# Two layers of a DeltaNet and Conformer encoder: gates stored as sigmoids, running sums one tile sooner, squares, weights and stores moved

## The chip, the core and the metric

The kernel runs on one core of a Trainium2 chip, as one launch. The metric is the device time of one execution in microseconds (us), the median of several runs. TensorE multiplies matrices, VectorE (DVE) and ScalarE (ACT) work on elements, GpSimd (POOL) takes some element work and stores, SyncE (SP) issues most of the loads. ScalarE and GpSimd issue DMAs too, each in the order of its own instructions.

## What is computed

Two layers, each a residual block on x of 2048 tokens by 1024 channels in float32; a final RMSNorm follows. Cut to what matters:

```python
h = rms_norm(x, norm_w)
qkv, z_a, a_lg, b_lg, cf_val, cf_glu, z_b, gate_lg = split(h @ w_in)
qkv = silu(depthwise_conv_centred(qkv, qkv_conv_w))
# 4 heads, both directions, chunked gated delta rule, running sums of g in a chunk
o = o_fwd + o_bwd
y_a = (rms_norm(o, dn_norm_w) * silu(z_a)) @ w_dn_out
u = depthwise_conv_centred(cf_val * sigmoid(cf_glu), cf_conv_w) + cf_conv_b
u = silu(layer_norm(u, cf_ln_w, cf_ln_b))
y_b = (u * silu(z_b)) @ w_cf_out
gate = sigmoid(gate_lg + gate_b)
x = x + (gate[0] * y_a + gate[1] * y_b) @ w_out
```

## The kernel before, in words

Channels lie on partitions, tokens on the free axis, in four blocks of 512. A product by a weight tile of 128 columns is three matmuls for each 128 of depth: weight and activation are each split in a high and a low part (`split`, L158 on ScalarE makes the high part, L159 on VectorE the low one), and L175, L176 and L177 multiply high by high, low by high, high by low. A tile of full depth is thus 24 matmuls of 128x512. TensorE's order is made of such tiles, and other work is put between them.

Each layer has these stages. **Projection**: for each of four heads, `head` makes the tiles of k, q and v with their convolution of five taps (`conv_tiles`: L563 on ScalarE, L565 on VectorE, then SiLU, L552) and `conformer` a tile of the conformer branch (GLU: L725 and L729). The follow-up work of a head is a queue of generators, `post`: at each tile `follow` runs the first of them up to its next `yield`. For head 0 the first is `scalars`, the decays and write strengths: long element work on VectorE (L444 to L470), then the running sums as two products (L475, L477), copied by L479, and their transpose L495. Behind it come `keys` (transposes of k and q, L573, sums of squares, Gram products L628 and L629, and the factors bh, L642) and `values`. Behind those, work of VectorE that is not tied to a tile lies in another queue, `back`, which `pump` feeds at a rate: `solve`, the inverse of the triangular blocks of a head (it starts with the transpose L666 of bh, its copy L668, a store and a load back, then steps L704, L706), and `conformer_conv`, 30 steps of L740.

**Gates**: `gates(0)` makes the 16 gate tiles for the blocks 0 and 1, 32 tiles; ScalarE adds the bias (L820, tile `go`) and stores them to `gt_d` in device memory. `conformer_norm` (L775 to L798) runs beside them. **Scan**: `delta` runs 16 steps of both directions in lockstep; a step has products such as L979 and L982, and `finish` norms and stores the outputs of earlier steps (squares L1034, L1052, L1057, and L1058 on VectorE). Between the parts of a step `pull` takes matmuls out of a `filler`: first `gates(1)` for blocks 2 and 3, then `early_merge`, the conformer's output product for blocks 0 and 1 times its gate: loads of `gt_d` (tile g), the sigmoid L1187 on ScalarE and L1193 on VectorE. The order of the scan is bound on every engine as it is written (`bind`). **Merge**: `merge` takes the other gates from `gt_d` (sigmoid L1247), multiplies, adds and makes the product with w_out; in the first layer L1297 adds x, `add_square` (L228, L231 on ScalarE) sums squares, and SyncE stores the new x (L149); in the second `last_out` does this and closes each block with the final norm.

Elsewhere a scheduler orders the instructions of each engine by their dependencies, so a line that is moved can move others.

Of the kernel before, what the change touches and what calls it, by code (L numbers as in the profile page):

```python
# [6 lines left out]
F32 = mybir.dt.float32  # L7
# [26 lines left out]
PART = 5  # L34
LATE = 4
AHEAD = 4
R2 = 3.7
# [25 lines left out]
def cut(x):  # L63
    return x.rearrange("p (a i) -> p a i", a=2)
# [13 lines left out]
class Trunk:  # L78
# [9 lines left out]

    def bind(self, start):
        last = {}  # L90
        for ins in self.nc.cur_bb.bb.instructions[start:]:
            if ins.engine in BOUND:
                if ins.engine in last:
                    self.tc.add_manual_dep(ins, last[ins.engine], NOSYNC, reason="written order")
                last[ins.engine] = ins.name
# [64 lines left out]

    def weight(self, src, kk):
        hi = self.pw.tile([P, KD, P], F32R, tag="whi", bufs=2, name="whi")[:, 0:kk, :]
        lo = self.pw.tile([P, KD, P], F32R, tag="wlo", bufs=2, name="wlo")[:, 0:kk, :]
        for k in range(0, kk, 4):
            raw = self.pw.tile([P, 4, P], F32, tag="wraw", bufs=2, name="wraw")
            self.load(raw, src[:, k:k + 4, :])
            self.split(hi[:, k:k + 4, :], lo[:, k:k + 4, :], raw)
        return hi, lo

# [256 lines left out]
    def scalars(self, pt):  # L426
# [42 lines left out]
        v_.tensor_copy(dch(self.beta), cdh(n(9)))  # L469
        yield  # L470
        yield
# [329 lines left out]
    def gates(self, half):  # L801
# [5 lines left out]
        for i, (j, b) in enumerate(seq):  # L807
            for q, _ in seq[i:]:
                if q not in ws and len({z for z, _ in seq[i:] if z in ws}) < 2:
                    ws[q] = self.weight(self.a["w_in"][self.l, 28 + q], KD)  # L810
            blk = 2 * half + b
            ps = self.pd()
            for more in self.dense_steps(ps, ws[j], self.hx(blk), KD):
                if more:
                    yield 1
            if self.rate:
                self.follow()
                self.pump(self.rate)
            o = self.st("go")
            nc.scalar.activation(cut(o), sort(ps), AF.Identity, bias=self.vec[:, V_GB + j:V_GB + j + 1])  # L820
            self.astore(self.gt_d[j, :, blk * NB:(blk + 1) * NB], o)
            yield 1

    def delta(self):
# [272 lines left out]
        for step in range(NCH):  # L1097
# [27 lines left out]
            if step == NCH - 1:  # L1125
                break
            next(new)
            pull(STEP[2])
            next(last)
            ready = go(step + 1)  # L1130
# [46 lines left out]
    def early_merge(self, wcf, ahead, seq, gs, gate):  # L1177
        nc = self.nc
        for i, (j, b) in enumerate(seq):
            if b == 0:  # L1180
                wc = ahead
                if j + 1 < KD:
                    ahead = self.weight(wcf[j + 1], 4)
            if i + 2 < len(seq):
                gate(i + 2)
            g = gs.popleft()
            nc.scalar.activation(g, g, AF.Sigmoid)  # L1187
            sl = slice(b * NB, (b + 1) * NB)
# [25 lines left out]
    def merge(self, l, xd, fnw):  # L1214
# [10 lines left out]
        for half in range(2):  # L1225
# [10 lines left out]
            for j in range(KD):  # L1236
# [5 lines left out]
                for b in order:  # L1242
# [3 lines left out]
                    self.load(gt[:, 0:n], self.gt_d.rearrange("(n j) p t -> j p n t", n=2)[j][:, 0:n, tk])  # L1246
                    nc.scalar.activation(gt[:, 0:n], gt[:, 0:n], AF.Sigmoid)  # L1247
                    ys[b] = [gt[:, 0, :], gt[:, 1, :] if half else self.y1[:, j, b * NB:(b + 1) * NB]]
# [28 lines left out]
            for j in range(KD):  # L1277
# [12 lines left out]
                for b in order:  # L1290
# [7 lines left out]
                    self.add_square(ss[:, sl], xn[j][:, sl], j == 0)  # L1298
                    self.store(xnew[j, :, tk], xn[j][:, sl])
                if j + 1 < KD:  # L1300
# [22 lines left out]
    def last_out(self, l, half, xd, fnw, yhi, ylo, ahead, order, w0):  # L1323
# [42 lines left out]
        for b in order:  # L1366
# [15 lines left out]
            for j in range(whole):  # L1382
# [7 lines left out]
                if whole < KD and j and len(ws) < KD - whole:  # L1390
# [3 lines left out]
                    ws.append((hi, lo))  # L1394
            if whole == KD:
                if b == order[0]:
                    w0 = self.weight(a["w_out"][l, 0], KD)
                run(close(o, NB, None))
                continue
# [81 lines left out]
```

## Time and profile before

| | us |
|---|---|
| median of 3 runs | 3178.48 (3176.97 to 3181.95) |
| the profiled execution | 3177.78 |
| its span | 3176.0 |
| TensorE busy | 3087.8 |
| VectorE busy | 2400.1 |
| ScalarE busy | 1382.5 |
| GpSimd busy | 298.4 |

The span goes from the first to the last instruction that the profiler saw. An engine's busy time is the union of its instructions; TensorE's holds the stretches at a lower clock too, which the granted clock (PEclk, a share of full speed) shows. A wait is idle time of an engine, put down to the instruction that ended it.

### The profile page before, as it was taken

To read this page: it belongs to the slowest core of one execution; us is meant where nothing else is said; L and a number is where in the kernel's file an instruction comes from. 1 tells how busy PE (TensorE), PEld (TensorE's weight loads), DVE (VectorE), ACT (ScalarE), POOL (GpSimd) and SP (SyncE) were. 2 spreads that over 40 slices of the span, in tenths; PEclk is the share of its full clock that TensorE was granted. 3 is DMA by queue.
4 is the path that set the end of the run, shared out by engine and by line. 5 is a ranking of instruction groups with operands and counts; after the bars stand their busy time and mean duration, and the time that the engine had idled before them with its cause. 6 is when DMAs were issued, how large, how long until landed. Compare 5 with 4: busy or idle time off the path is not lost. (4 is left out here: it accounts for less than half of the span.)

```text
span 3176.0 us, 51511 instructions
## 1 busy us (share of the span) xinstructions
PE 3087.8 (97%) x19190; PEld 2715.3 (85%) x19190; DVE 2400.1 (76%) x4441; ACT 1382.5 (44%) x3113; POOL 298.4 (9%) x297
## 2 busy tenths in 40 slices
PE   6998999999999999999999999999999999999998
PEld 5887888888889998888888888888888899988887
DVE  7769899997656698746667699998955667877665
ACT  5624252522344466533345332525234445765342
POOL 3000000000022222000000000000001222200000
PEclk9998999999999999999999999999999999999999
DMA  4232323234588787665413141414356878965643
GB/s 145 83 100 70 100 80 101 82 100 161 184 295 251 253 265 226 192 195 135 144 44 114 49 124 64 120 60 120 115 171 231 278 238 265 289 191 188 215 157 126
DMA packets 429418, 501.72 MB, mean 158 GB/s; under 512 B 96432, under 2 KB 262960, under 8 KB 429168
## 3 DMA queue, kind: packets, MB, share of 16 engines
q1 hardware_dynamic: 355840, 388.58, 39.9%
q10 hardware_dynamic: 65264, 80.09, 7.3%
q0 software_dynamic: 8064, 29.76, 2.5%
q8 instruction: 151, 2.47, 0.3%
q14 instruction: 99, 0.81, 0.1%
HBM read 342.74 MB, written 155.58 MB: 157 GB/s over the span
## 5 line engine op out<-in xcount | busy, mean ns | idle before, releaser
L175 PE MATMUL pd<-h,whi 128*128 128x512 f32 x2816 | 1093.7, 389 | 0.0
L177 PE MATMUL pd<-h,wlo 128*128 128x512 f32 x2816 | 1071.5, 381 | 4.9 <-DVE wlo L159 4.9
L176 PE MATMUL pd<-h,whi 128*128 128x512 f32 x2816 | 1072.1, 381 | 0.0
L740 DVE SCALAR_TENSOR_TENSOR cacc<-gp,vec,cacc 128x1009 f32<-128x1009 f32 (+1 forms) x480 | 615.8, 1283 | 31.1 <-ACT cacc L738 28.1
L177 PEld LDWEIGHTS pd<-h,wlo 128*128 128x128 f32 x2816 | 534.7, 190 | 82.6 <-DVE wlo L159 6.5
L175 PEld LDWEIGHTS pd<-h,whi 128*128 128x128 f32 x2816 | 534.7, 190 | 80.0 <-issue 1.4
L176 PEld LDWEIGHTS pd<-h,whi 128*128 128x128 f32 x2816 | 535.4, 190 | 72.9 <-issue 1.9
L158 ACT ACTIVATE whi<-wraw 128x512 fp32r<-128x512 f32 x394 | 240.2, 624 | 451.0 <-PE pd L176 302.9
L159 DVE TENSOR_TENSOR wlo<-wraw,whi 128x512 fp32r<-128x512 f32 x394 | 270.4, 699 | 135.4 <-ACT whi L158 135.0
L565 DVE SCALAR_TENSOR_TENSOR acc<-cin,vec,acc 128x1022 f32<-128x1022 f32 (+1 forms) x192 | 245.7, 1299 | 11.5 <-ACT acc L563 10.5
L177 PE MATMUL pd<-yhi,wlo 128*128 128x512 f32 x488 | 185.7, 381 | 4.5 <-DVE wlo L159 4.5
L175 PE MATMUL pd<-yhi,whi 128*128 128x512 f32 x488 | 185.5, 380 | 1.8 <-ACT whi L158 1.8
L176 PE MATMUL pd<-ylo,whi 128*128 128x512 f32 x488 | 185.0, 379 | 0.0
L820 ACT ACTIVATE go<-pd,vec 128x512 f32<-128x512 f32 x128 | 87.0, 680 | 123.7 <-PE pd L177 101.7
L541 ACT ACTIVATE cin<-pd 128x512 f32<-128x512 f32 x96 | 56.7, 592 | 165.5 <-PE pd L177 165.4
L752 ACT ACTIVATE ao<-pd 128x512 f32<-128x512 f32 x64 | 38.3, 599 | 179.2 <-PE pd L177 174.5
L177 PEld LDWEIGHTS pd<-yhi,wlo 128*128 128x128 f32 x488 | 92.2, 189 | 19.8 <-DVE wlo L159 6.9
L175 PEld LDWEIGHTS pd<-yhi,whi 128*128 128x128 f32 x488 | 92.2, 189 | 15.7 <-ACT whi L158 3.0
L175 PE MATMUL pd<-uop,whi 128*128 128x512 f32 x256 | 100.5, 393 | 3.2 <-ACT dm L1052 3.2
L176 PEld LDWEIGHTS pd<-ylo,whi 128*128 128x128 f32 x488 | 92.2, 189 | 13.0
L176 PE MATMUL pd<-uop,whi 128*128 128x512 f32 x256 | 98.2, 383 | 0.0
L177 PE MATMUL pd<-uop,wlo 128*128 128x512 f32 x256 | 97.8, 382 | 0.0
(311 smaller groups left out, 4837.1 us busy)
## 6 DMA issues: line engine op xcount, KB each, us to landing
wraw<-w_in SPq DMA_DIRECT2D x240, 256.0 KB, 3.5
gt<-go ACTq DMA_DIRECT2D x128, 256.0 KB, 4.1
dl<-gr SPq DMA_DIRECT2D x128, 256.0 KB, 5.3
dl<-kq SPq DMA_DIRECT2D x64, 512.0 KB, 6.4
dl<-kv SPq DMA_DIRECT2D x64, 512.0 KB, 5.8
wraw<-w_out SPq DMA_DIRECT2D x90, 256.0 KB, 3.1
kq<-acc SPq DMA_DIRECT2D x16, 1024.0 KB, 5.3
gr<-go ACTq DMA_DIRECT2D x64, 256.0 KB, 2.2
```

The lines of the kernel that those rows point to most:

```text
L158: self.nc.scalar.activation(hi, src, AF.Copy)
L159: self.nc.vector.tensor_tensor(out=lo, in0=src, in1=hi.bitcast(F32), op=ALU.subtract)
L175: mm(ps, whi[:, k, :], xhi, start=k == 0, stop=False)
L176: mm(ps, whi[:, k, :], xlo, start=False, stop=False)
L177: mm(ps, wlo[:, k, :], xhi, start=False, stop=k == kk - 1)
L541: nc.scalar.activation(cut(t[:, o + b * NB:o + (b + 1) * NB]), sort(ps), AF.Copy)
L565: self.nc.vector.scalar_tensor_tensor(out=out, in0=t[:, k:k + n], scalar=wc(k), in1=out, op0=ALU.mult, op1=ALU.add)
L740: self.nc.vector.scalar_tensor_tensor(out=acc, in0=t[:, k:k + n], scalar=wc(k), in1=acc, op0=ALU.mult, op1=ALU.add)
L752: nc.scalar.activation(cut(o), sort(ps), func)
L820: nc.scalar.activation(cut(o), sort(ps), AF.Identity, bias=self.vec[:, V_GB + j:V_GB + j + 1])
```

## The change

It has six parts. `gates` stores the sigmoid of the gates of blocks 0 and 1, and the two places that read them leave out theirs. In the steps from 12 on, the squares of a pair of outputs are written behind the third `pull`. One of two yields in `scalars` goes. The first w_out tile of a block in `last_out` is written between the parts of the closing norm, whose VectorE order is bound. In `early_merge` the loads of the next w_cf tile and its split are written apart, one for each block. `merge` stores the new x from ScalarE's queue.

```diff
--- before.py
+++ after.py
@@ -33,6 +33,7 @@
 Z = '121'
 PART = 5
 LATE = 4
+LATE_SQUARES = 12
 AHEAD = 4
 R2 = 3.7
 BIG = -1.0e30
@@ -86,10 +87,10 @@
     def mark(self):
         return len(self.nc.cur_bb.bb.instructions)
 
-    def bind(self, start):
+    def bind(self, start, engines=BOUND):
         last = {}
         for ins in self.nc.cur_bb.bb.instructions[start:]:
-            if ins.engine in BOUND:
+            if ins.engine in engines:
                 if ins.engine in last:
                     self.tc.add_manual_dep(ins, last[ins.engine], NOSYNC, reason="written order")
                 last[ins.engine] = ins.name
@@ -158,14 +159,23 @@
         self.nc.scalar.activation(hi, src, AF.Copy)
         self.nc.vector.tensor_tensor(out=lo, in0=src, in1=hi.bitcast(F32), op=ALU.subtract)
 
-    def weight(self, src, kk):
+    def weight_parts(self, src, kk):
         hi = self.pw.tile([P, KD, P], F32R, tag="whi", bufs=2, name="whi")[:, 0:kk, :]
         lo = self.pw.tile([P, KD, P], F32R, tag="wlo", bufs=2, name="wlo")[:, 0:kk, :]
+        raws = []
         for k in range(0, kk, 4):
-            raw = self.pw.tile([P, 4, P], F32, tag="wraw", bufs=2, name="wraw")
-            self.load(raw, src[:, k:k + 4, :])
-            self.split(hi[:, k:k + 4, :], lo[:, k:k + 4, :], raw)
-        return hi, lo
+            raws.append(self.pw.tile([P, 4, P], F32, tag="wraw", bufs=2, name="wraw"))
+            self.load(raws[-1], src[:, k:k + 4, :])
+
+        def split():
+            for k, raw in zip(range(0, kk, 4), raws):
+                self.split(hi[:, k:k + 4, :], lo[:, k:k + 4, :], raw)
+        return (hi, lo), split
+
+    def weight(self, src, kk):
+        w, split = self.weight_parts(src, kk)
+        split()
+        return w
 
     def dense_steps(self, ps, w, xs, kk):
         mm = self.nc.tensor.matmul
@@ -468,7 +478,6 @@
         v_.reciprocal(out=n(9), in_=n(9))
         v_.tensor_copy(dch(self.beta), cdh(n(9)))
         yield
-        yield
         ps = self.pz()
         tri = self.st("tri")[:, 0:256].rearrange("p (d c) -> p d c", d=2)
         v_.tensor_scalar(out=tri, in0=self.con[:, C_MF:C_MB + 1, :], scalar1=0.0, scalar2=None, op0=ALU.is_equal)
@@ -817,7 +826,8 @@
                 self.follow()
                 self.pump(self.rate)
             o = self.st("go")
-            nc.scalar.activation(cut(o), sort(ps), AF.Identity, bias=self.vec[:, V_GB + j:V_GB + j + 1])
+            nc.scalar.activation(cut(o), sort(ps), AF.Identity if half else AF.Sigmoid,
+                                 bias=self.vec[:, V_GB + j:V_GB + j + 1])
             self.astore(self.gt_d[j, :, blk * NB:(blk + 1) * NB], o)
             yield 1
 
@@ -1124,8 +1134,11 @@
             done.clear()
             if step == NCH - 1:
                 break
-            next(new)
+            if step < LATE_SQUARES:
+                next(new)
             pull(STEP[2])
+            if step >= LATE_SQUARES:
+                next(new)
             next(last)
             ready = go(step + 1)
             last = new
@@ -1180,11 +1193,12 @@
             if b == 0:
                 wc = ahead
                 if j + 1 < KD:
-                    ahead = self.weight(wcf[j + 1], 4)
+                    ahead, split = self.weight_parts(wcf[j + 1], 4)
+            elif j + 1 < KD:
+                split()
             if i + 2 < len(seq):
                 gate(i + 2)
             g = gs.popleft()
-            nc.scalar.activation(g, g, AF.Sigmoid)
             sl = slice(b * NB, (b + 1) * NB)
             ps = self.pd()
             for more in self.dense_steps(ps, wc, lambda k: (self.u0[:, k, sl], self.u0[:, 4 + k, sl]), 4):
@@ -1244,7 +1258,8 @@
                     gt = self.hm("gt")[:, 0:2 * NB].rearrange("p (n t) -> p n t", n=2)
                     n = 1 + half
                     self.load(gt[:, 0:n], self.gt_d.rearrange("(n j) p t -> j p n t", n=2)[j][:, 0:n, tk])
-                    nc.scalar.activation(gt[:, 0:n], gt[:, 0:n], AF.Sigmoid)
+                    if half:
+                        nc.scalar.activation(gt[:, 0:n], gt[:, 0:n], AF.Sigmoid)
                     ys[b] = [gt[:, 0, :], gt[:, 1, :] if half else self.y1[:, j, b * NB:(b + 1) * NB]]
                 if half:
                     for b in order:
@@ -1296,7 +1311,7 @@
                     self.load(xr, xd[j][:, tk])
                     v_.tensor_tensor(out=cut(xn[j][:, sl]), in0=sort(ps), in1=cut(xr), op=ALU.add)
                     self.add_square(ss[:, sl], xn[j][:, sl], j == 0)
-                    self.store(xnew[j, :, tk], xn[j][:, sl])
+                    self.astore(xnew[j, :, tk], xn[j][:, sl])
                 if j + 1 < KD:
                     w = self.weight(a["w_out"][l, j + 1], KD)
             if half:
@@ -1393,9 +1408,13 @@
                         self.split(hi[:, k:k + 4, :], lo[:, k:k + 4, :], raws[len(ws)][:, k:k + 4, :])
                     ws.append((hi, lo))
             if whole == KD:
+                c = close(o, NB, None)
+                run(c, 2)
+                start = self.mark()
                 if b == order[0]:
                     w0 = self.weight(a["w_out"][l, 0], KD)
-                run(close(o, NB, None))
+                run(c)
+                self.bind(start, (mybir.EngineType.DVE,))
                 continue
             start = self.mark()
             n = NB // 2
```

Line numbers of the changed kernel are 9 to 14 higher. The places where the instructions move:

VectorE, the running sums of the first layer (`scalars`; abw holds its work, ngc, neg and sig go with the decays), before:

```order
L464 COPY abw<-abw 128x16x2x4
L479 COPY abw<-pz 128x128
L481 COPY abw<-pz 128x128
L483 TENSOR_SCALAR ngc<-abw 128x128
L487 TENSOR_SCALAR neg<-eg 128x128
L490 TENSOR_TENSOR abw<-abw 128x128
L496 COPY abw<-pz 128x128
L159 TENSOR_TENSOR wlo<-wraw,whi 128x512
L498 TENSOR_SCALAR abw<-abw,sig 128x128
```

and now:

```order
L474 COPY abw<-abw 128x16x2x4
L488 COPY abw<-pz 128x128
L490 COPY abw<-pz 128x128
L492 TENSOR_SCALAR ngc<-abw 128x128
L505 COPY abw<-pz 128x128
L507 TENSOR_SCALAR abw<-abw,sig 128x128
L496 TENSOR_SCALAR neg<-eg 128x128
L499 TENSOR_TENSOR abw<-abw 128x128
L574 SCALAR_TENSOR_TENSOR acc<-cin,vec,acc 128x1022 x2
```

The copy of the transposed sums (L496, now L505) and its product come ahead of two splits (L159), and the convolution of the first head follows at once.

VectorE, the start of the first head's solve (L666's result is copied by L668, now L677; sol is the solve's buffer, cacc the conformer's convolution), before:

```order
L740 SCALAR_TENSOR_TENSOR cacc<-gp,vec,cacc 128x1009 x8
L511 MEMSET cin 128x2
L688 TENSOR_TENSOR sol<-gr 128x1024
L511 MEMSET cin 128x2
L693 TENSOR_TENSOR sol<-sol 128x1024
L159 TENSOR_TENSOR wlo<-wraw,whi 128x512 x2
L668 COPY bt<-pz 32x128
L159 TENSOR_TENSOR wlo<-wraw,whi 128x512 x2
L694 TENSOR_TENSOR sol<-sol,br 64x1024
L695 TENSOR_TENSOR sol<-sol,br 64x1024
```

and now:

```order
L651 TENSOR_TENSOR bh<-beta,rk 128x32
L521 COPY gp<-gp 128x30
L653 COPY beta<-bh 128x32
L697 TENSOR_TENSOR sol<-gr 128x1024
L663 TENSOR_TENSOR vo<-pz,vs 128x512 x4
L677 COPY bt<-pz 32x128
L518 MEMSET cin 128x2
L749 SCALAR_TENSOR_TENSOR cacc<-gp,vec,cacc 128x1009 x3
```

The copy stood behind the conformer's first convolution; now it follows bh and the four products vo, and the convolution follows it. On TensorE the transpose L666 stands behind matmul 736 of the layer before and behind matmul 472 now.

ScalarE in the last steps of the scan (oss are the sums of squares, g the gates, dm and dh buffers), before:

```order
L915 ACTIVATE dh_6988<-dh_6988 32x4x32 x4
L1034 ACTIVATE junk,oss<-dm_6984 128x128 x8
L158 ACTIVATE whi<-wraw 128x512
L1187 ACT_TABLE_LOAD
L1187 ACTIVATE g_10748<-g_10748 128x512
L1187 ACTIVATE g_10896<-g_10896 128x512
L988 ACTIVATE dm_6983<-pz,eg 128x128 x8
```

and now:

```order
L925 ACTIVATE dh_6988<-dh_6988 32x4x32 x4
L1044 ACTIVATE junk,oss<-dm_6984 128x128 x8
L159 ACTIVATE whi<-wraw 128x512
L998 ACTIVATE dm_6983<-pz,eg 128x128 x8
L939 ACTIVATE dh_6989<-pz 128x128
L1007 ACTIVATE dm_6983<-pz 128x512 x2
```

The table load and both sigmoids have left; the squares stand where they stood. VectorE at the same place, before:

```order
L917 TENSOR_TENSOR dl_6981<-dl_6981,dm_6982 128x512 x2
L919 TENSOR_TENSOR dl_6981<-dl_6981,dm_6982 128x512 x2
L159 TENSOR_TENSOR wlo<-wraw,whi 128x512
L1193 TENSOR_TENSOR y_11062<-pd,g_10748 128x512
L1058 SCALAR_TENSOR_TENSOR dh_6985<-pz,vec,dh_6985 128x512
L1058 SCALAR_TENSOR_TENSOR dh_6986<-pz,vec,dh_6986 128x512
L961 COPY dl_6981<-pz 64x4x64
L962 COPY dl_6981<-pz 64x4x64
```

and now:

```order
L927 TENSOR_TENSOR dl_6981<-dl_6981,dm_6982 128x512 x2
L929 TENSOR_TENSOR dl_6981<-dl_6981,dm_6982 128x512 x2
L1207 TENSOR_TENSOR y_11053<-pd,g_10739 128x512
L1068 SCALAR_TENSOR_TENSOR dh_6985<-pz,vec,dh_6985 128x512
L1068 SCALAR_TENSOR_TENSOR dh_6986<-pz,vec,dh_6986 128x512
L971 COPY dl_6981<-pz 64x4x64
L972 COPY dl_6981<-pz 64x4x64
L160 TENSOR_TENSOR wlo<-wraw,whi 128x512
```

L1193 (now L1207) is ahead of L159 (now L160), which was ahead of it. On ScalarE's whole order there are 60 table loads before and 85 now.

## Rows read from the trace of the kernel before

**Rows 1.** The page: its first line, and part 1, busy time of each engine.

```profile
span 3176.0 us, 51511 instructions
...
PE 3087.8 (97%) x19190; PEld 2715.3 (85%) x19190; DVE 2400.1 (76%) x4441; ACT 1382.5 (44%) x3113; POOL 298.4 (9%) x297
```

**Rows 2.** TensorE's waits over the whole span: total us, times, longest us.

```profile
PE pz L573 <- ACT acc L552: 14.9, 2, 8.3
...
PE pz L979 <- DVE dh L1058: 8.5, 2, 4.2
...
PE pz L201 <- DVE ss L232: 1.9, 1, 1.9
```

**Rows 3.** Windows: length; busy us (instructions) of PE, PEld, DVE, ACT, POOL; PEclk, DMA share, GB/s.

```profile
152.70:310.10 157.40, 147.20 (x714) 129.17 (x713) 126.16 (x200) 56.71 (x129) 7.05 (x10) 0.95 0.28 86
1707.00:1861.20 154.20, 145.73 (x714) 128.16 (x713) 125.53 (x200) 56.75 (x129) 7.04 (x10) 0.97 0.29 88
208.00:233.00 25.00, 25.00 (x118) 21.82 (x117) 2.96 (x5) 4.79 (x9) 0.78 (x3) 1.00 0.29 97
272.00:288.00 16.00, 9.85 (x31) 8.18 (x32) 16.00 (x26) 9.55 (x38) 0.00 (x0) 0.50 0.75 207
1824.00:1840.00 16.00, 9.32 (x35) 7.99 (x36) 16.00 (x26) 9.62 (x38) 0.00 (x0) 0.68 0.71 201
```

**Rows 4.** VectorE's timeline, 175 to 234: start, us, operation, [idle before, releaser].

```profile
175.09 0.22 DVE L642 TENSOR_TENSOR bh<-beta,rk 128x32 f32<-128x32 f32 x1
...
224.54 0.28 DVE L668 COPY bt<-pz 32x128 f32<-32x128 f32 x1 [14.98 <-PE pz L666]
...
233.61 1.22 DVE L694 TENSOR_TENSOR sol<-sol,br 64x1024 f32<-64x1024 f32 x1 [7.09 <-DMA br<-bp]
```

**Rows 5.** TensorE's timeline: the L573 of head 0's v and of head 1.

```profile
165.44 1.04 PE L573 MATMUL pz<-con,acc 128*128 128x128 f32 x8
...
171.50 1.04 PE L573 MATMUL pz<-con,acc 128*128 128x128 f32 x8
...
276.25 3.68 PE L573 MATMUL pz<-con,acc 128*128 128x128 f32 x16 [8.30 <-ACT acc L552]
```

**Rows 6.** ScalarE's timeline, 1234 to 1238, the end of the first layer's scan.

```profile
1234.93 0.61 ACT L158 ACTIVATE whi<-wraw 128x512 fp32r<-128x512 f32 x1
1235.56 1.28 ACT L1187 ACT_TABLE_LOAD   x1
1236.86 1.15 ACT L1187 ACTIVATE g<-g 128x512 f32<-128x512 f32 x2
```

**Rows 7.** VectorE's timeline, the same place.

```profile
1232.90 1.29 DVE L919 TENSOR_TENSOR dl<-dl,dm 128x512 f32<-128x512 f32 x2
...
1237.52 0.69 DVE L1193 TENSOR_TENSOR y<-pd,g 128x512 f32<-128x512 f32 x1 [1.25 <-ACT g L1187]
1238.12 1.40 DVE L1058 SCALAR_TENSOR_TENSOR dh<-pz,vec,dh 128x512 f32<-128x512 f32 x2
```

**Rows 8.** TensorE's timeline, the same place.

```profile
1238.92 1.44 PE L979 MATMUL pz<-dh,dl 128*128 128x128 f32 x5 [4.23 <-DVE dh L1058]
```

**Rows 9.** Windows, as rows 3: three scan steps from one L1057 to the next, then 1425 to 1450.

```profile
1205.37:1228.47 23.10, 23.10 (x249) 21.03 (x248) 18.97 (x53) 18.18 (x57) 4.54 (x4) 1.00 1.03 354
1228.47:1258.26 29.79, 25.56 (x250) 23.11 (x249) 23.75 (x63) 17.11 (x57) 4.55 (x4) 0.89 0.48 127
2781.99:2811.11 29.12, 24.89 (x250) 22.38 (x248) 23.48 (x63) 17.24 (x57) 4.55 (x4) 0.94 0.41 132
1425.00:1450.00 25.00, 23.09 (x108) 19.83 (x107) 15.29 (x38) 7.70 (x11) 0.00 (x0) 0.93 0.49 133
```

**Rows 10.** Groups of line L796: its instructions, and what ended ScalarE's idle time before them.

```profile
L796 ACT ACTIVATE lnc<-lnc,vec x32: 794/800/815, 806.4 to 2448.4; 128x512 f32<-128x512 f32 x32
...
  DVE lnc L793: 22.3, 8
```

**Rows 11.** Waits of SyncE's DMA queue over the span, the row of the stores of xn.

```profile
SPq L149 <- DVE xn L1297: 69.8, 23, 4.6
```

## The prediction, made before the changed kernel was run

> **What bounds the kernel now.** I read the page's head first: of a span of 3176.0 us TensorE is busy 3087.8 [rows 1], so only 88.2 us of idle time can be had, and with it what a lower clock adds inside the busy time. Next the waits of TensorE, which say who ended that idle time [rows 2]: 14.9 us in two waits of L573 (the transposes of a head's q and k) for ScalarE's SiLU of L552, 8.5 us in two waits of L979 (first product of a scan step) for VectorE's L1058, 1.9 us at L201. The windows then show what such a wait costs beyond itself [rows 3]: head 0 to head 1 in the first layer, from 152.70 to 310.10, holds 10.2 us of idle time, and behind it in 272 to 288 the granted clock is 0.50, the 1.2 GHz level, where TensorE had stood without work before it fell. The same place in the second layer is 1707.00 to 1861.20, 8.5 us idle, clock 0.68 in 1824 to 1840.
>
> The cause lies some 60 us earlier, on VectorE. From 208 to 233 it works 2.96 us of 25 [rows 3]. It waits 14.98 us for one transpose (L666, whose result L668 copies), then 7.09 us for the DMA that brings that result back [rows 4]. Its input bh had been made at 175.09 [rows 4]; the transpose came late only because it stands late in TensorE's order. VectorE then has the solve of head 0 and the convolution of head 1 at once, and L573 starts at 276.25 after 8.30 us of waiting [rows 5].
>
> **The change part by part.** *One yield less* moves the running sums and all that follows in that queue of side work one 24-matmul tile earlier. A tile is some 5.2 us: the two L573 x8 at 165.44 and 171.50 are 6.06 apart [rows 5], and their eight transposes take about 0.9 of it. In the built order L666 of head 0 moves far more, from behind matmul 736 to behind 472, the second layer's likewise; the solve's steps then fill VectorE's empty 22 us, and head 1's L573 stand spread over five tiles as they do for heads 2 and 3, instead of sixteen in a bunch. I take the whole loss of the two places: first layer 10.2 idle plus half of the 9.85 us that ran at 0.50, 15.1; second layer 8.5 idle plus 0.32 of 9.32 us, 3.0, together 11.5 [rows 3]. Sum 26.6. The new place of L666 asks bh sooner: TensorE reaches it at 171.50 + 1.04 - 5.2 = 167.4, where bh came at 175.09 before [rows 4, 5]. In between stood thirteen of the conformer's L740, which the new order puts behind bh, so I expect no wait; the bound is 175.3 - 167.4 = 7.9 us a layer. The sums themselves may hold TensorE for a part of a tile. I take 25 as the gain, between 26.6 and 26.6 - 15.8 = 10.8, near the upper end, as bh loses some 13 us of work ahead of it.
>
> *Gates stored as sigmoids.* At the end of the scan the chain is ScalarE's split, then a table load of 1.28 us, then the sigmoid g at 1236.86 [rows 6], VectorE's L1193 at 1237.52 waiting 1.25 for it, L1058 behind it [rows 7], and TensorE's L979 after 4.23 us [rows 8]. That step lasts 29.79 us where the one before it lasts 23.10, in the second layer 29.12 [rows 9], an excess of 6.7 and 6.0. Without the sigmoid L1193 can start when L919 ends, 1232.90 + 1.29 = 1234.2 [rows 7]; it waits for nothing else new (wlo now stands behind L962). L1193 0.6 and the two L1058 1.4 make 1236.1, of which L979's first operand needs one half, so TensorE waits some 0.9 to 1.4 us instead of 4.23, and the clock should hardly fall. Gain 12.7 less 2 x 1.3, about 10. The 32 sigmoids of 0.62 us in the merge are off TensorE's path otherwise and count nothing: ScalarE is busy 44% of the span.
>
> The sigmoids now run when the gates are made, and ScalarE goes back and forth between tables: its order holds 60 table loads before and 85 after, 25 x 1.28 = 32 us of ScalarE [rows 6]. Ten of the new ones stand at the gates, six more at the GLU (L725), three at L552, the rest at other places. At each of the eight norms ScalarE waits 22.3 / 8 = 2.8 us for L793, then runs four L796 of 0.80 [rows 10], now with a load on either side: 2.8 + 3.2 + 2.6 = 8.6 us in which no gate tile is taken away. Three accumulators of a tile each, some 10 us after the last one was freed, cover this; if that cover is gone, it is up to 8.6 - 5.2 = 3.4 us a norm. Taken: 1 us in all, between 0 and 8 x 3.4 = 27.
> By rows a load costs 1.28 and nothing more: the split ends at 1234.93 + 0.61, the load starts at 1235.56 and the sigmoid 1.30 later [rows 6]. The Trainium skill (ScalarE: Activation LUTs, on table loads) gives a switch of sets as that load plus a drain, about 2.66 us in all. That would be 25 x 2.66 = 66 us of ScalarE; the trace does not agree.
>
> *New x by ScalarE's queue.* 32 stores of the first layer leave SyncE, where they held later loads 69.8 us waiting for L1297 [rows 11], loads of xr and of weights among them, and go behind squares on ScalarE that wait for the same xn. ScalarE pays about 0.35 us each (11 us, beside TensorE's work). The place to gain is 1425 to 1450: L201 waits 1.9 us and the clock is 0.93, another 1.75 us [rows 2, 9]. I take 2 of these 3.7; bounds 0 and 3.7, and below nothing up to a loss of 2 should the squares come late.
>
> *Late squares, split weights, output weights ahead.* In the built order the squares of L1034 stand where they stood in the steps that count, and the split of w_out moves by a few places in one block. The waits there are 0.4 to 1.4 us; I take 0, bounds minus 1.5 and plus 2.
>
> Sum against the profiled execution: 3177.8 - 25 - 10 - 2 + 1 = 3141.8. That execution is 0.7 under the median of the three runs, 3178.5, so **3142**.
>
> **The rivals.** (1) *The stall halves.* VectorE has now the wait for the vo transposes behind bh, before the conformer's convolution starts, so that some of the gap of 208 to 233 is spent there, and head 1's second half comes late again by half. For it: VectorE's margin is about 10 us (22 saved, some 10 idle before the first L740). Against: heads 2 and 3 go through the same order without such a wait. It gives 3142 + 12 = 3154. (2) *The yield does not bring it*: TensorE waits a tile for the sums or bh and head 1 stays as it was. Then only 12 of the gains stand and 1 is paid: 3167. For it: the sums' chain on VectorE ends only at its place; bh came at 175.09. Against: bh was late for work that has moved away. (3) *Slower, by the tables.* If the accumulators are not free when ScalarE's block begins, each of the eight norms holds TensorE for that block less half a tile, 8.6 - 2.6 = 6.0 us; 8 x 6.0 = 48 us outweigh all the rest: 3142 - 1 + 48 = 3189. It decides from (3178.5 + 6.4 - 3141) / 8 = 5.5 us a norm. For it: ScalarE works in order, and 20 of the loads and waits come in pairs there. Against: in before 6.0 us of the same block (2.8 + 3.2) cost TensorE next to nothing there, and 2.6 more leaves the cover of 10. The Trainium skill's 2.66 (same page and section) would make the block 2.8 + 3.2 + 5.3 = 11.3 us, past that cover. No row bears the larger figure out.
>
> **How the numbers follow.** Forecast 0.74, the stall halves 0.12, the yield does not bring it 0.08, the tables 0.03, something else 0.03. The range: below, all bounds met, 3177.8 - 26.6 - 12.7 - 3.7 - 2, about 3133, less 1 for run to run; above it takes in rival 1 and most of rival 2, 3166. A measurement of this kernel tells 0.2%, 6.4 us, from no change. Faster needs a time under 3172: forecast, rivals 1 and most of 2, 0.90; within 0.2% 0.05; slower 0.05.
>
> **What would show it.** Right: L573 of head 1 without a wait over 2 us, clock 1.00 in what was 268 to 288, VectorE's L668 without its 15 us; the scan's fifteenth step near 24.5 us, with no table load in it; L201 behind the merge under 1 us. TensorE's idle time near 60 us. Wrong: a wait of L573 for L552 that stays (rivals 1, 2), a wait of TensorE for bh or the sums (2), waits of TensorE for go of L820 or for dg of L212 between 718 and 1100 (3), or L979 waiting still for L1058, with y then late for another reason.

## The result, and the profile after

The changed kernel takes 3142.74 us (median of 4, 3141.69 to 3144.99), the kernel before 3180.22 in the same series; the ratio is 0.9882, 95% interval 0.9865 to 0.9900, 37 us less. The forecast was 3142. The profiled execution took 3143.1 us.

The page and TensorE's waits of the changed kernel, against [rows 1, 2] (L185 to L187 are the matmuls L175 to L177, L159 and L160 the splits, L989 is L979, L211 is L201, L224 is L214):

```profile
span 3141.3 us, 51438 instructions
...
PE 3077.3 (98%) x19190; PEld 2707.1 (86%) x19190; DVE 2400.3 (76%) x4441; ACT 1377.3 (44%) x3074; POOL 297.9 (9%) x297
```

```profile
PE pz L224 <- DVE dg L222: 11.1, 7, 3.3
PE pd L187 <- DVE wlo L160: 6.0, 5, 1.7
PE pd L185 <- ACT whi L159: 5.8, 4, 2.7
...
PE pz L989 <- DVE dh L1068: 1.6, 2, 0.8
...
PE pz L211 <- DVE ss L242: 0.5, 1, 0.5
```

L573's waits are gone, L979's are down from 8.5 us to 1.6. Idle time is 64 us (span less busy) where it was 88. The third row, the wait for the high parts of weights, has grown: the kernel before has 1.8 us of it in two waits.

Windows, with the columns of [rows 3, 9]: VectorE's former gap, the stretch that ran at 0.50, and the fifteenth scan step of both layers:

```profile
208.00:233.00 25.00, 25.00 (x118) 21.89 (x117) 24.02 (x51) 4.05 (x7) 0.57 (x1) 1.00 0.30 103
```

```profile
268.00:288.00 20.00, 20.00 (x104) 17.66 (x103) 20.00 (x19) 13.73 (x46) 0.00 (x0) 1.00 0.48 137
```

```profile
1215.97:1240.38 24.41, 23.59 (x249) 21.11 (x248) 22.61 (x63) 12.27 (x45) 4.53 (x4) 1.00 0.52 159
2752.70:2777.10 24.40, 23.59 (x249) 21.10 (x248) 22.62 (x63) 12.26 (x44) 4.55 (x4) 1.00 0.49 154
```

VectorE works 24.0 of the 25 us in which it worked 3.0, TensorE does not stop behind it, the granted clock stays at 1.00, and the step of 29.79 us takes 24.41. VectorE's timeline shows why there is no gap (L651 is L642, L677 is L668, L703 is L694):

```profile
158.01 0.20 DVE L651 TENSOR_TENSOR bh<-beta,rk 128x32 f32<-128x32 f32 x1
160.97 1.23 DVE L697 TENSOR_TENSOR sol<-gr 128x1024 f32<-128x1024 f32 x1 [2.53 <-DMA gr<-go]
...
168.73 0.27 DVE L677 COPY bt<-pz 32x128 f32<-32x128 f32 x1
...
194.85 1.21 DVE L703 TENSOR_TENSOR sol<-sol,br 64x1024 f32<-64x1024 f32 x1
```

bh comes 17 us sooner than in [rows 4], its transpose is copied at 168.7 without a wait where it was 224.5, and the solve goes on at 194.9 instead of 233.6. The running sums themselves do not start sooner: their first product (L475, now L484) starts at 123.3 before and at 123.8 now, both times after a wait of 1.24 us for VectorE's abw. What comes sooner is the transpose of the sums (L495, now L504; 125.2 instead of 128.8) and all that follows it. "The sooner sums" below means that.

A ledger by stage makes the runs comparable. Each number of a stage is the difference of two starts in a trace, in us: *heads* from the running sums (L475) to the first gate tile (L820), *gates* from there to the 37th, *step* the fifteenth scan step, each for the first and second layer. The median is over all executions of a kernel, and the ratio is to the kernel before in the same series; the stages come from the one profiled execution, which lies up to 7 us off the median (`yield_squares` 3150.3, `logits` 3137.4).

| kernel | heads | gates | step | median | ratio to before, interval |
|---|---|---|---|---|---|
| before | 595.3, 592.6 | 200.8, 203.3 | 29.8, 29.1 | 3180.2 | |
| changed | 581.1, 580.9 | 202.9, 206.6 | 24.4, 24.4 | 3142.7 | 0.9882 (0.9865 to 0.9900) |
| yield_only | 581.0, 580.9 | 204.4, 202.5 | 30.4, 29.2 | 3153.5 | 0.9919 (0.9904 to 0.9933) |
| yield_back | 595.4, 592.4 | 208.8, 209.7 | 24.4, 24.4 | 3177.4 | 0.9993 (0.9984 to 1.0003) |
| solve_first | 594.6, 594.3 | 201.2, 205.7 | 30.3, 29.7 | 3180.9 | 1.0008 (0.9995 to 1.0021) |
| conv_first | 587.6, 587.8 | 203.8, 206.9 | 24.4, 24.4 | 3156.4 | 0.9931 (0.9916 to 0.9946) |
| logits | 580.5, 580.9 | 203.6, 203.2 | 24.2, 24.2 | 3142.1 | 0.9876 (0.9860 to 0.9892) |
| squares_early | 580.4, 580.9 | 205.6, 204.7 | 24.4, 24.4 | 3142.3 | 0.9880 (0.9865 to 0.9894) |
| store_sp | 581.1, 580.9 | 202.1, 203.6 | 24.4, 24.4 | 3141.1 | 0.9873 (0.9858 to 0.9888) |
| tables_more | 580.5, 580.9 | 208.8, 210.5 | 24.4, 24.4 | 3149.7 | 0.9900 (0.9884 to 0.9917) |
| neither | 581.2, 580.9 | 206.0, 202.8 | 28.6, 27.1 | 3152.4 | 0.9917 (0.9896 to 0.9938) |
| yield_squares | 580.5, 580.9 | 207.5, 205.8 | 24.8, 24.8 | 3143.4 | 0.9887 (0.9856 to 0.9917) |
| yield_sigmoid | 581.0, 580.9 | 201.7, 204.7 | 26.9, 25.4 | 3144.4 | 0.9896 (0.9869 to 0.9922) |
| three_parts | 580.9, 580.9 | 208.3, 202.6 | 24.2, 24.2 | 3146.1 | 0.9896 (0.9875 to 0.9917) |

Of the 34.7 us between the two spans the heads gave 14.2 + 11.7 = 25.9 and the two steps 5.4 + 4.7 = 10.1; the gates took 2.1 + 3.3, and the rest gave some 4. Heads and steps repeat to 0.8 us in kernels that share the code there; the gate stage scatters between 202 and 208 us in kernels with the yield out, with and without the stored sigmoids, so single numbers of it mean little.

### The profile page after: what moved, and what is told of

It is laid out like the page before. It is cut to its first block, busy times and chain, and to the rows that moved or that the text cites. A ratio compares the mean times of both kernels' runs of the same rounds, so it can differ in the third digit from the quotient of the medians.

```text
span 3141.3 us, 51438 instructions
## 1 busy us (share of the span) xinstructions
PE 3077.3 (98%) x19190; PEld 2707.1 (86%) x19190; DVE 2400.3 (76%) x4441; ACT 1377.3 (44%) x3074; POOL 297.9 (9%) x297
## 5 line engine op out<-in xcount | busy, mean ns | idle before, releaser
L185 PE MATMUL pd<-h,whi 128*128 128x512 f32 x2816 | 1092.3, 388 | 0.0
L187 PE MATMUL pd<-h,wlo 128*128 128x512 f32 x2816 | 1070.5, 380 | 1.5 <-DVE wlo L160 1.5
L185 PEld LDWEIGHTS pd<-h,whi 128*128 128x128 f32 x2816 | 534.1, 190 | 79.5 <-issue 1.4
L187 PEld LDWEIGHTS pd<-h,wlo 128*128 128x128 f32 x2816 | 533.7, 190 | 78.6 <-DVE wlo L160 2.3
L159 ACT ACTIVATE whi<-wraw 128x512 fp32r<-128x512 f32 x394 | 239.3, 623 | 478.6 <-PE pd L186 352.6
L160 DVE TENSOR_TENSOR wlo<-wraw,whi 128x512 fp32r<-128x512 f32 x394 | 267.8, 693 | 116.9 <-ACT whi L159 115.2
L187 PE MATMUL pd<-yhi,wlo 128*128 128x512 f32 x488 | 185.6, 380 | 4.6 <-DVE wlo L160 4.5
L185 PE MATMUL pd<-yhi,whi 128*128 128x512 f32 x488 | 185.5, 380 | 0.7 <-ACT whi L159 0.7
L187 PEld LDWEIGHTS pd<-yhi,wlo 128*128 128x128 f32 x488 | 92.2, 189 | 19.5 <-DVE wlo L160 6.6
L185 PE MATMUL pd<-uop,whi 128*128 128x512 f32 x256 | 100.2, 391 | 5.1 <-ACT whi L159 5.1
L185 PEld LDWEIGHTS pd<-yhi,whi 128*128 128x128 f32 x488 | 92.2, 189 | 14.3 <-ACT whi L159 1.5
L187 PE MATMUL pd<-uop,wlo 128*128 128x512 f32 x256 | 98.0, 383 | 0.1
```

The source lines that it names most:

```text
L159: self.nc.scalar.activation(hi, src, AF.Copy)
L160: self.nc.vector.tensor_tensor(out=lo, in0=src, in1=hi.bitcast(F32), op=ALU.subtract)
L185: mm(ps, whi[:, k, :], xhi, start=k == 0, stop=False)
L187: mm(ps, wlo[:, k, :], xhi, start=False, stop=k == kk - 1)
```

## The experiments

**The yield alone, and all but the yield.** `yield_only` is the kernel before without that line, `yield_back` the changed kernel with it:

```diff
         v_.tensor_copy(dch(self.beta), cdh(n(9)))
         yield
-        yield
```

> The kernel before with the one yield of the running sums taken out and nothing else changed. Theory (the yield carries the gain of the heads): the waits of L573 for L552 in both layers are gone, TensorE's period from head 0 to head 1 falls by some 14 us in the first layer and 12 in the second, and the whole falls by 25 to 27 us, to about 3153; the scan's fifteenth step stays at 29.8 and 29.1 us. Rival (the parts need each other, or the gain came from the sigmoids and stores): less than 10 us, above 3168.

> The changed kernel with that yield put back. Theory: the bunched L573 and its waits of 8 and 6.5 us return, the clock falls behind them as before, and the time is 25 to 27 us above the changed kernel, about 3169. Rival (another part of the change also clears that place): under 3155.

`yield_only` gives 3153.5 us, 24 less than its kernel before, with heads as in the changed kernel and steps as before: the theory holds. `yield_back` has the heads of the kernel before, as expected, and the short steps, but 3177.4 us, 8 more than expected. The ledger has them in the gates, 8.0 and 6.4 us more than before. Its waits, and behind them the first of these rows in the kernel before:

```profile
PE pz L224 <- DVE dg L222: 20.1, 10, 3.5
PE pz L583 <- ACT acc L562: 15.7, 2, 8.4
```

```profile
PE pz L214 <- DVE dg L212: 9.6, 6, 3.3
```

The norm's L224 waits 20.1 us in ten places, where the changed kernel has 11.1 in seven. In the gate stages alone it waits 11.2 us here (3.16 and 2.78 us, then 1.72 and 3.50), 2.9 in the kernel before and 3.6 in the changed one, whose norms stand one tile sooner. So with the norms at their old place the other five parts cost about what the scan gains, and only with the yield out do they pay. Which of the five costs it there was not tried.

**Is it the order in the queue?** With the yield out, the solve of head 0 enters the queue `back` ahead of the conformer's first convolution. Two kernels change that order alone, the first on the kernel before, the second on the changed one:

```diff
-        self.back.append(self.solve(hd, bh))
+        (self.back.append if hd else self.back.appendleft)(self.solve(hd, bh))
```

```diff
-            self.back.append(self.conformer_conv(j, half, t))
+            (self.back.append if j or half else self.back.appendleft)(self.conformer_conv(j, half, t))
```

> The kernel before, its two yields kept, with only the solve of head 0 put at the front of the queue of work that is not tied to a tile, ahead of the conformer's first convolution. Theory (what the yield does is to let that solve enter the queue ahead of the convolution; the sums being a tile sooner is worth nothing by itself): the transpose L666 stands a tile behind its place in the changed kernel, the L573 waits are gone, and the time falls by 22 to 27 us, about 3155. Rival (the sums must be sooner): the waits of L573 stay over 4 us in each layer and the time stays above 3168.

> The changed kernel, its sums a tile sooner, with only the conformer's first convolution put at the front of that queue, ahead of the solve of head 0. Theory (order in the queue): L675, as L666 is called there, comes some 210 matmuls later, VectorE waits for it again and then for the DMA of its result, the waits of L573 come back in part or whole, and the time is 15 to 27 us above the changed kernel, 3158 to 3170. Rival (the earlier sums alone give the gain): within 5 us of the changed kernel, under 3148.

`solve_first` gains nothing: this theory fell. Its rival had the time right and the waits wrong: L573 no longer waits, but TensorE stops for the low half of weights, in the first layer here (4.14 and 6.68 us in the second):

```profile
208.28 0.79 PE L177 MATMUL pd<-h,wlo 128*128 128x512 f32 x1 [3.36 <-DVE wlo L159]
243.31 0.79 PE L177 MATMUL pd<-h,wlo 128*128 128x512 f32 x1 [5.93 <-DVE wlo L159]
```

VectorE's timeline of that kernel shows what stood ahead of the second:

```profile
239.86 0.19 DVE L706 TENSOR_TENSOR sol<-sol,solt 128x31 f32<-128x31 f32 x1
240.08 1.22 DVE L708 TENSOR_TENSOR sol<-sol,br 64x1024 f32<-64x1024 f32 x1
241.31 1.22 DVE L709 TENSOR_TENSOR sol<-sol,br 64x1024 f32<-64x1024 f32 x1
242.56 1.29 DVE L159 TENSOR_TENSOR wlo<-wraw,whi 128x512 fp32r<-128x512 f32 x2
```

The solve starts 10 us later than in the changed kernel (first L704 at 208.1 against 197.9), ends 2.7 us later, and its last steps run in one piece with the split behind them. The granted clock is 0.86 in 200 to 225 and again in 225 to 250. The wait has moved and costs the same.

`conv_first` takes 13.6 us more than the changed kernel, a little under what its theory named and far over its rival. It loses half of the heads' gain, 6.5 and 6.8 us, and L573 waits 3.65 us again in each layer. VectorE's old gap is back in part:

```profile
215.55 0.28 DVE L677 COPY bt<-pz 32x128 f32<-32x128 f32 x1 [4.08 <-PE pz L675]
222.25 1.22 DVE L703 TENSOR_TENSOR sol<-sol,br 64x1024 f32<-64x1024 f32 x1 [6.42 <-DMA br<-bp]
```

So both count: the sooner sums with the convolution first are worth half, the solve first without the sooner sums nothing, the two together all.

**What frees the fifteenth step?** Five kernels take the parts that touch it apart. `logits` undoes the sigmoids in the changed kernel, `squares_early` the squares, `neither` both:

```diff
-            nc.scalar.activation(cut(o), sort(ps), AF.Identity if half else AF.Sigmoid,
-                                 bias=self.vec[:, V_GB + j:V_GB + j + 1])
+            nc.scalar.activation(cut(o), sort(ps), AF.Identity, bias=self.vec[:, V_GB + j:V_GB + j + 1])
...
+            nc.scalar.activation(g, g, AF.Sigmoid)
...
-                    if half:
-                        nc.scalar.activation(gt[:, 0:n], gt[:, 0:n], AF.Sigmoid)
+                    nc.scalar.activation(gt[:, 0:n], gt[:, 0:n], AF.Sigmoid)
```

```diff
-LATE_SQUARES = 12
+LATE_SQUARES = 16
```

> The changed kernel with the gates of blocks 0 and 1 stored as logits again, the sigmoids back in the filler and in the merge. Theory (the sigmoid holds the scan's last full step): that step is 29 to 30 us again in both layers, 10 us lost; 17 of the table loads leave the gates and the norms, which gives back the 1.2 and 2.4 us that the gate stage lost; together 5 to 8 us above the changed kernel, about 3149. Rival (the order of VectorE and the late squares free that step, not the sigmoid): the step stays under 26 us and the time is at or under the changed kernel.

> The changed kernel with the squares of the late steps written where they were (the bound 12 set to 16, so that no step takes the new place). The changed kernel's trace has new waits of TensorE for ScalarE's split L159 behind these squares, 1.34 and 1.04 us at the end of the first scan and 2.73 at the end of the second. Theory (the late squares cause these and free nothing): the waits go or halve, 1 to 3 us under the changed kernel, about 3140. Rival (the late squares are what lets the fifteenth step end sooner): that step gets longer by over 2 us in each layer, over 3146.

> The changed kernel with the sigmoids back in filler and merge and with the squares of the late steps where they were; the sooner sums, the split weights, the stores and the last product stay. Each of the two undone alone left the fifteenth step at 24.2 to 24.4 us. Theory (each is enough alone: the first takes the sigmoid out of the chain, the second lets it run ahead of the squares): with both undone ScalarE ends its squares near 4.6 us before the place where L1187 ended before, then loads its table and makes g, L979 waits some 3.5 us again and the step lasts 28 to 29 us in both layers, in all 6 to 9 us above the changed kernel. Rival (the split of the weights frees the step, since it takes VectorE's L159 out of the way): the step stays under 26 us.

In `logits` the step is 24.2 us, so the step does not need the sigmoid away; the rival was right. ScalarE's timeline there:

```profile
1217.75 1.26 ACT L924 ACTIVATE dh<-dh 32x128 f32<-32x128 f32 x4 [3.23 <-DVE dh L916]
1219.02 1.28 ACT L1201 ACT_TABLE_LOAD   x1
1220.31 0.63 ACT L1201 ACTIVATE g<-g 128x512 f32<-128x512 f32 x1
1224.18 0.61 ACT L159 ACTIVATE whi<-wraw 128x512 fp32r<-128x512 f32 x1
```

Load and sigmoid go ahead of the eight squares, which fill 1220.9 to 1224.2, and g is there at 1220.9, before VectorE asks for it at 1221.55. In `squares_early` the squares are ahead again but there is no sigmoid: 24.4. The waits for the high parts of weights do not go with the late squares either (5.4 us against 5.8), so that theory fell. The traces point at the split weights instead: at the end of each scan TensorE waits 1.9 to 2.8 us for high parts in five kernels that write load and split apart (the changed one, `logits`, `squares_early`, and below `neither` and `three_parts`), and has no such wait there in the kernel before, `yield_only`, `yield_squares` and `yield_sigmoid`, which do not. With both undone, `neither`:

```profile
1223.50 1.28 ACT L1201 ACT_TABLE_LOAD   x1
1224.79 0.63 ACT L1201 ACTIVATE g<-g 128x512 f32<-128x512 f32 x1
```

```profile
1226.86 1.16 PE L988 MATMUL pz<-dh,dl 128*128 128x128 f32 x8 [3.71 <-DVE dh L1067]
```

The step lasts 28.6 and 27.1 us, the second less than the 28 to 29 expected, the wait is 3.71 where some 3.5 was expected, and the whole is 3152.4, 10 more than the changed kernel where 6 to 9 was expected. The profiled execution is only 5 above that of the changed kernel: its two steps are 6.9 longer, and the rest of the 10 is not seen in a trace. Each of the two parts is enough alone, given the split weights. Two kernels ask whether it also is with the weights split as before: `yield_squares` is `yield_only` with the diff below and `LATE_SQUARES = 12`, `yield_sigmoid` is `yield_only` with the gate lines of `logits` the other way round.

```diff
-            next(new)
+            if step < LATE_SQUARES:
+                next(new)
             pull(STEP[2])
+            if step >= LATE_SQUARES:
+                next(new)
```

> The kernel before with two edits, the one yield taken out and the squares of the late steps put behind the filling; gates as logits, weights split as before. Theory (late squares let split and sigmoid go ahead; VectorE's L159 still stands ahead of L1193): the step lasts 24.5 to 25.5 us, the gates and norms cost what they did before, and the time is that of the changed kernel to 3 us, about 3143. Rival (the split of the weights is needed): the step lasts over 27 us, about 3149.

> The kernel before with two edits, the one yield taken out and the gates of blocks 0 and 1 stored as sigmoids; squares and weights as before. In its order VectorE's L159 stands ahead of L1193 and waits for ScalarE's split behind the eight squares. Theory: L979 waits 2.5 to 3 us, the step lasts 26.5 to 27.5 us in both layers, about 4 us under the kernel with the yield alone. Rival (the sigmoid's leaving is enough, as the prediction had it): the step lasts 24.4 us and it is 10 us under.

`yield_squares` has steps of 24.8 us, as its theory said; its four times run from 3131.7 to 3150.3, so its median of 3143.4 says little. `yield_sigmoid` has steps of 26.9 and 25.4, of which only the first is in its theory's range; its median, 9 us under `yield_only`, lies between its theory's 4 and its rival's 10, and the intervals leave both open. VectorE's timeline there, and then TensorE's wait in the same step:

```profile
1220.35 1.29 DVE L918 TENSOR_TENSOR dl<-dl,dm 128x512 f32<-128x512 f32 x2
1223.02 0.69 DVE L159 TENSOR_TENSOR wlo<-wraw,whi 128x512 fp32r<-128x512 f32 x1 [1.38 <-ACT whi L158]
1223.63 0.68 DVE L1191 TENSOR_TENSOR y<-pd,g 128x512 f32<-128x512 f32 x1
1224.23 1.40 DVE L1057 SCALAR_TENSOR_TENSOR dh<-pz,vec,dh 128x512 f32<-128x512 f32 x2
```

```profile
1224.07 1.16 PE L978 MATMUL pz<-dh,dl 128*128 128x128 f32 x8 [1.93 <-ACT dm L987]
```

The split of the weights stands ahead of y, and waits for ScalarE behind the squares. TensorE's L978 (L979), however, starts before L1057 (L1058), when ScalarE's L987 (L988) is done, in both layers. So the longer steps show that without the split weights a stored sigmoid brings only a part, and late squares nearly all; that VectorE's order is the reason is not shown, nor why TensorE waits for another instruction here.

**The stores, and what is enough.** `store_sp` puts the stores of the new x back on SyncE; `three_parts` is the kernel before with the yield out, the late squares and the split weights only:

```diff
-                    self.astore(xnew[j, :, tk], xn[j][:, sl])
+                    self.store(xnew[j, :, tk], xn[j][:, sl])
```

> The changed kernel with the stores of the new x back on SyncE's queue. Theory: L201 behind the merge (L211 in the changed kernel) waits about 1.9 us again instead of 0.54 and the clock falls there; 2 to 4 us above the changed kernel, all of it between 1280 and 1620 us. Rival (the sums of squares came sooner for another reason): the merge takes the same time to 0.5 us, and that wait stays under 1 us.

> The kernel before with three edits: the yield taken out, the squares of the late steps behind the filling, and loads and split of w_cf written apart. Left out are the sigmoids stored, ScalarE's queue for the new x and the weights ahead in the last product. Theory (these three parts carry all of the gain): the changed kernel's time to 3 us, 3139 to 3145, with steps of 24.2 us. Rival (one of the parts left out carries 4 us or more): over 3147.

`store_sp` is at 3141.1 us, its wait of L211 for ss is 0.3 us, and from the last L1067 of the first scan to the second layer's sums it takes 384.4 us against 384.7 in the changed kernel: the store's queue brought nothing that the runs can tell, the rival holds. The wait is 0.5 us in `yield_only` too, whose stores were never moved. `three_parts` takes 3146.1, between what the theory and its rival named; its interval holds the changed kernel's ratio, and its steps and heads are the changed kernel's. The run can't tell whether the parts left out are worth nothing or some 4 us; the weights ahead in the last product were not tried alone.

**More table loads.** A SiLU of one column is added behind every second gate tile of blocks 0 and 1:

```diff
+            if not half and b == 0:
+                nc.scalar.activation(self.junk[:, 0:1], o[:, 0:1], AF.Silu)
```

> The changed kernel with one more ScalarE instruction behind every second gate tile of blocks 0 and 1, a SiLU of one column into a scratch tile, which makes ScalarE change its table there and back: 56 more table loads in its order, 72 us by 1.28 us each. Theory (such loads lie beside TensorE's work as long as the accumulators are covered): at most 6 us above the changed kernel, with the waits of TensorE still at the four norms of a layer. Rival (each load ends on the path): 50 to 72 us above it. A rule of 2.66 us a switch would make 56 of them 149 us, past what ScalarE has free in the gate stage, and the loads would show a pause of 1.38 us behind each.

3149.7 us, 7 more than the changed kernel for 72 us of loads, where the theory allowed 6; the intervals of the two overlap. The waits of L224 grow, at one norm in each layer, to 5.73 and 6.94 us; elsewhere the loads lie beside TensorE's work. ScalarE's timeline shows one switch there and back:

```profile
747.10 0.69 ACT L829 ACTIVATE go<-pd,vec 128x512 f32<-128x512 f32 x1 [2.25 <-PE pd L187]
747.82 0.33 ACTq L153 DMA_DIRECT2D gt<-go  x1
748.18 1.28 ACT L833 ACT_TABLE_LOAD   x1 [0.39 <-ACT go L829]
749.47 0.20 ACT L833 ACTIVATE junk<-go 128x1 bf16<-128x1 f32 x1
...
757.44 1.28 ACT L829 ACT_TABLE_LOAD   x1
758.73 0.69 ACT L829 ACTIVATE go<-pd,vec 128x512 f32<-128x512 f32 x1
```

The operation follows its load at once, with no pause of 1.38 us. At the first of the two there are 0.39 us between the end of the gate and the load, in which ScalarE issues the store of the gate.

No version beats the changed kernel by more than the runs can tell; `logits` and `store_sp` are level with it.

## Why the prediction was right

The time was forecast within 1 us, and the two large terms held; that it came so near is in part luck, since the gates took 5.4 us where 1 was forecast and the rest gave some 4 where 2 was. *The heads*: 25 us forecast, 25.9 in the ledger (14.2 and 11.7 where the whole loss was priced at 15.1 and 11.5), and `yield_only` shows them to come from that one line. The steps of that term held as well: VectorE's gap filled, L668 without its wait, the L573 spread, and the loss priced as idle time plus the slow stretch behind it. The wait for bh that the bound of 7.9 us a layer covered did not come: bh is there at 158.0, and its transpose starts at 167.7. The second rival (the yield does not bring it) and the first (half) are out, though `conv_first` shows that half was what the sums alone would have given. Two things the prediction did not see. The sums do not move: TensorE reaches their product at the same place and waits 1.24 us for abw in both kernels, and only what follows comes sooner. And the place of the solve by itself is worth nothing; `solve_first` kept the whole loss as a new wait for L177.

*The step*: forecast a wait of 0.9 to 1.4 us and a gain of 10; measured 0.82 and 0.81, and 10.1. The lower bound was added up a little high: with half of the two L1058 its own terms give 1234.2 + 0.6 + 0.7 - 1234.7 = 0.8, where 1234.7 is the start of L979 without its wait. The price was right, but the reason given was only one of two. The prediction put it all on the stored sigmoid and took the late squares and the split weights at 0, because the squares stand where they stood in the changed order. They do only because the sigmoid has left: with it in place (`logits`) the moved squares free the chain. And the sum for the sigmoid already used the split weights, as it let L1193 follow L919 with wlo behind L962; without them (`yield_sigmoid`) the step is 26.9 and 25.4 us. Taking the part away is the test that an order of instructions can't replace.

*The tables*: 1 us forecast; the gate stage took 5.4 us more in the profiled execution, but kernels without the stored sigmoids (`yield_only`, `three_parts`) show 202 to 208 us there too, so the runs do not show a cost of these loads, nor that it is 0. Not all 25 new loads are the sigmoids': `yield_only` has 67 where the kernel before has 60, so 7, the added ones at the GLU and at L552 among them, come with the yield, and 18 with the sigmoids (`logits` 67, the changed kernel 85). `tables_more` bears out most of the cover, some 7 us for 72 us of loads, and the third rival is out in this form; `yield_back` shows that with the norms a tile later the gate stage does lose 14 us, the place that rival named at a third of the size, though no run separates the sigmoids from the other parts there. The Trainium skill (ScalarE: Activation LUTs, What ACT_TABLE_LOAD costs) gives 2.66 us for a switch of sets, load and drain. The traces do not agree: the load takes 1.28 us and the next operation starts at once.

*The stores* were taken at 2 us; the wait of L201 they were meant to end is gone without them, and no gain of theirs is seen. Late squares and split weights were taken at 0; where the other parts are missing the first are worth 7.3 us of step over both layers (`neither` against `logits`) and the second 3.5 (`yield_sigmoid` against `squares_early`). In each of these two, some 1.5 us is a lower clock in the first layer alone.

## What to carry to other kernels

Where several edits clear the same wait, each of them can look worthless when it is undone alone (24.2 and 24.4 us here) and worth most of the gain when it is done alone (24.8): undo them in pairs before one is called useless or the cause. An engine that is idle for 20 us while another is the bound is worth reading: the work that it could have done there came back later here as a wait and a lower clock. Moving that work by itself can move the wait onto what is queued behind it, so its cost is known only with the order of that engine's other work.

## What the runs showed that was not expected

The parts of the change that touch the gate stage go with more or less time in it by where the norms stand: 208.8 and 209.7 us with the norms at their old place, 202.9 and 206.6 a tile sooner, in one execution each.

After the wait of L573 for 8.30 us the granted clock stood at 0.50, the 1.2 GHz level, in 272 to 288 [rows 3]; in the scan steps of the changed kernel, with waits of 0.82 us, it stayed at 1.00. In between, a wait of one length did not always cost the same. In `neither` L979 waits 3.71 us in the first layer and 3.70 in the second, with the same work in both, and the steps are 1.5 us apart by the clock alone:

```profile
1216.93:1245.55 28.62, 24.91 (x249) 22.26 (x248) 22.88 (x63) 16.82 (x55) 4.54 (x4) 0.94 0.42 132
2752.75:2779.83 27.08, 23.38 (x250) 21.10 (x249) 22.50 (x63) 15.72 (x49) 4.57 (x4) 1.00 0.45 140
```

`yield_sigmoid` shows the same: 1.93 us of waiting in either layer, a clock of 0.94 and then 1.00, steps of 26.9 and 25.4. What decides between the two is not shown, so the price of such a wait is known here only to 1.5 us.
